# Input products are emitted as soon as a PSUM bank is free; only their evacuation waits for the phase and the places that the job needs

## The chip, the cores and the metric

One core of one Trainium2 chip runs the whole kernel in one launch. The metric is the device time of the launch in microseconds (us), the median of three runs. PE is the matrix engine, DVE the vector engine, ACT the scalar engine, POOL the general one (GpSimd), SP the engine whose queue issues nearly all DMAs.

## The reference

One layer of a streaming encoder on 2048 prompt rows and 32 sample rows of width 1024, in f32. Cut to what matters here:

```
h = layer_norm(x)
p = h @ w_in                      # 1024 -> 6160 columns: all "input products"
A: q, k, v, z of 8 heads x 64     # softmax over a band of 9 chunks of 64 keys, + learned bias
B: q, k, v, z, a, b of 8 heads    # conv of width 4 + SiLU, then gated DeltaNet in chunks of 64
                                  #   (a triangular solve per chunk, a state carried chunk to chunk)
ya = (attention * silu(zA)) @ w_branch_a
yb = (rms_norm(delta) * silu(zB)) @ w_branch_b
y  = layer_norm(ALPHA*h + (sigmoid(gA)*ya + sigmoid(gB)*yb) @ w_out)
```

The new keys, values, conv rows and states are outputs too.

## The kernel before

**Stages.** The prompt is cut in two halves of 1024 columns; the 32 sample columns ride with the second half. For each half the kernel computes the input products one block of 128 output features (a *job*) after the other, and beside them runs first phase 1 (branch B, `phase_b`) and then phase 0 (branch A, `phase_a`). So the stages in time are B of half 0, A of half 0, B of half 1, A of half 1, and last the merge with the two output projections. A few jobs, the merge gates, belong to no phase and are strewn in between as filler for PE.

**An input product.** A job's weights are split into f16 `whi` + `wlo`, and h lies as f16 `hi` + `lo`. One product block of 512 columns is 24 matmuls (`hi,whi`, `hi,wlo` eight times each, then `lo,whi` eight times) into one PSUM bank named `pj`, of which there are two. A job has two blocks in half 0 (512 + 512 columns) and three in half 1 (512 + 272 + 272). The job's `evac` then takes the bank to SBUF, mostly on ACT, and gives the bank back: `vf<-pj` for a v job of attention, `raw<-pj` for a conv job, `sig<-pj` for a gate job.

**What sets the order.** The instructions are written down by a list scheduler. Each piece of work is a Python generator (a *stream*) with a clock of its own; `Flow.run` always resumes the one whose clock is lowest, and `Engine.price` moves the clock on by a modelled cost. Streams wait for one another by `Gate` (a number of places, first come first served), `Mark` (an event) and `Queue`. The engines of the chip then run each their list in that order; what waits on the chip are the semaphores that the data need.

**The stream that writes the products** is `multiply`. It takes the next job with its split weights from `q_w`, in one fixed order. For a job of a phase (`job.key`) it then waits for `go`, which `enter` sets once the phase before is over, makes the job's `evac`, and waits for the job's places (`job.slots`). Only then does it ask for a bank (`bank["pj"]`) and emit the 24 matmuls. The places are `raw_slots` (two) for the three conv jobs of a head pair in branch B; `vf_slot` (one) and `vt_slots` (two) for v, `kst_slots` (two) for k, `q_slots` (two) for q and `z_slots` (one) for z of a head pair in branch A. While `multiply` waits, no later product can be emitted either, a filler's included.

**The other work that the text speaks of.** In branch B, `chain` carries the state over the chunks: per chunk five matmuls (`a<-state,k_bd`, `a<-state,q_bd`, `a<-r,u_bd`, `c<-vn,kd_bd`, `a<-vn,qk_bd`) with DVE and ACT steps between them, the last of which is `v_t<-a`. After eight chunks, `tail` normalises (`sqo` on ACT, `ms` on DVE and POOL, `v_t<-v_t,ms` on POOL), transposes on PE (`a<-ident,v_t`), and gates. In branch A, attention of a head pair is 8 tiles x 2 heads of scores (`a<-kst,qd` and `ql`), exponentials (`sb`), transposes (`b<-ident,sb`) and values (`c<-vt,ph` and `pl`). `job_v` ends with `rest`: the maximum of `vf`, its transposes into `vt` (`b<-ident,vs`), and in half 1 also the output rows (`b<-ident,vf`) one by one through the two `b` banks that attention uses too; its last step is the copy `v_s<-b`, after which `vf_slot` is given back.

Of the kernel before, what the change touches and what calls it, by code (L numbers as in the profile page):

```python
# [251 lines left out]
def trunk(ctx: ExitStack, tc: tile.TileContext, x_p, x_s, cache_k, cache_v, st_conv, st_gdn,  # L252
# [4 lines left out]
    flow = Flow()  # L257
# [20 lines left out]
    def mark():  # L278
        return Mark(flow)
# [8 lines left out]
    def pt(tag):  # L288

        return psum.tile([P, 512], F32, tag=tag, bufs=banks[tag], name=tag)  # L290
# [245 lines left out]
    def h_cols(half, c0, n):  # L536
        b = 0 if c0 < SPLIT else 1
        hi, lo = hT[half][b]
        o = c0 - b * SPLIT
        return hi[:, :, o:o + n], lo[:, :, o:o + n]  # L540


    class Job:
# [2 lines left out]

        def __init__(self, half, wid, src, evac=None, key=None, cols=P, blocks=None):
            self.wid = wid
            self.half, self.src, self.evac, self.cols, self.key, self.slots = half, src, evac, cols, key, ()
            self.end = self.two = False  # L550
            self.blocks = blocks or BLOCKS[half]

# [34 lines left out]
    def divide():  # L587

        while True:
# [16 lines left out]
            for i in range(2):  # L606
# [8 lines left out]
                    q_w.put((job, hi, lo))  # L615
                yield

    def multiply():

        while True:  # L620
            some, todo = [], [(0, 0)]
            while todo:
                bi, which = todo.pop(0)
                if which == len(some):
                    some.append((yield from q_w.get()))
                    job = some[which][0]
                    if which == 0:

                        todo = [(b, w) for b in range(len(job.blocks)) for w in range(1 + job.two)][1:]
                    if job.key:  # L630
                        go, make = phases[job.key[0]][job.half]
                        yield go
                        job.evac, job.slots = make[0](*job.key[1:])
                    for g in job.slots:
                        yield g
                job, wh, wl = some[which]
                c0, n, gcol = job.blocks[bi]
                tiles = range(c0 // P, (c0 + n + P - 1) // P)
                for i in tiles:
                    yield h_ready[job.half][i]  # L640
                hh, hl = h_cols(job.half, c0, n)
                yield bank["pj"]
                ps = pt("pj")
                for k in range(KD):
                    PE.matmul(ps[:, 0:n], wh[:, k], hh[:, k, :], start=(k == 0), stop=False)
                    yield
                    if job.cols == P:
                        PE.matmul(ps[:, 0:n], wl[:, k], hh[:, k, :], start=False, stop=False)
                        yield
                for i in tiles:  # L650
                    yield l_ready[job.half][i]
                for k in range(KD):
                    PE.matmul(ps[:, 0:n], wh[:, k], hl[:, k, :], start=False, stop=(k == KD - 1))
                    if k == KD - 1:
                        last = bi == len(job.blocks) - 1
                        if job.end and (bi == 0 or last):
                            h_free[0 if bi == 0 else 1].give()
                        if last:
                            w_gate.give()
                    yield  # L660
                flow.start(job.evac(bi, c0, n, gcol, ps))
                if job.end and job.half == 1:
                    if last:
                        jobs_done.done()
                        flow.start(leave())
# [34 lines left out]
    def leave():  # L700
        for _ in range(2):
            yield sig_slots
        yield front_w
        front_done.done()
# [1150 lines left out]
    phases = [[(mark(), []) for _ in range(2)] for _ in range(2)]  # L1855
# [304 lines left out]
    with tc.tile_pool(name="x0", bufs=1, reuse_waits="tile") as xp:  # L2160
        flow.start(norm_params(xp))
        flow.start(build_h(0, xp, 8))
        flow.start(fetch(marked()), 2.0)
        flow.start(setup(xp), 20.0)
        flow.start(setup2(xp), 30.0)
        flow.start(spread(), 100.0)
        flow.start(divide())
        flow.start(multiply())
        flow.run(l_ready[0][7])
    for half in range(2):  # L2170
        stack, make, done = phase_b(half)
# [9 lines left out]
        ap, stack, make, done = phase_a(half)  # L2181
# [66 lines left out]
```

## Time and profile before

| what | value |
|---|---|
| median of 3 runs | 2180.49 us (2174.0 to 2183.27) |
| the profiled execution: its time, its span | 2178.3 us, 2176.2 us |
| PE busy, matmuls | 2008.7 us (92%), 15098 |
| DVE / ACT / POOL busy | 1539.9 / 983.9 / 634.5 us |
| mean granted clock of PE | 0.971 |

The profiled execution is 2.2 us under the median. All work goes through two helpers, so nearly every row has the line L243 and is told apart by the tiles' names. PE's busy time is a union over pipelined matmuls: in a row of one instruction the time includes its overlap with the next, so the pace of a run of matmuls is read from a stretch of time, not from the mean of one.

### The profile page before, as it was taken

To read this page: it belongs to the slowest core of one execution; us is meant where nothing else is said; L and a number is where in the kernel's file an instruction comes from. 1 tells how busy PE (TensorE), PEld (TensorE's weight loads), DVE (VectorE), ACT (ScalarE), POOL (GpSimd) and SP (SyncE) were. 2 spreads that over 40 slices of the span, in tenths; PEclk is the share of its full clock that TensorE was granted. 3 is DMA by queue.
4 is the path that set the end of the run, shared out by engine and by line. 5 is a ranking of instruction groups with operands and counts; after the bars stand their busy time and mean duration, and the time that the engine had idled before them with its cause. 6 is when DMAs were issued, how large, how long until landed. Compare 5 with 4: busy or idle time off the path is not lost. (4 is left out here: it accounts for less than half of the span.)

```text
span 2176.2 us, 41392 instructions
## 1 busy us (share of the span) xinstructions
PE 2008.7 (92%) x15098; PEld 1436.2 (66%) x15098; DVE 1539.9 (71%) x4660; ACT 983.9 (45%) x2098; POOL 634.5 (29%) x708
## 2 busy tenths in 40 slices
PE   4898999999899999898999998899899998999998
PEld 4454665666465556565767776666676777988896
DVE  7689878874377657769887877437557577776676
ACT  5654545444366667554443533345556552111110
POOL 6343333322312123332233331310110214443333
PEclk9999999999999999999999999999999999999999
DMA  3223332332323223122223233231321526443331
GB/s 119 71 83 104 77 86 61 88 88 83 91 77 109 78 88 99 65 69 61 81 58 95 65 91 84 84 107 45 92 68 53 153 76 205 142 129 108 117 104 59
DMA packets 197719, 196.49 MB, mean 90 GB/s; under 512 B 79622, under 2 KB 147570, under 8 KB 197516
## 3 DMA queue, kind: packets, MB, share of 16 engines
q1 hardware_dynamic: 197516, 193.85, 30.4%
q8 instruction: 119, 1.95, 0.4%
q14 instruction: 84, 0.69, 0.1%
HBM read 135.91 MB, written 50.53 MB: 86 GB/s over the span
## 5 line engine op out<-in xcount | busy, mean ns | idle before, releaser
L243 PE MATMUL pj<-hi,whi 128*128 128x512 f16 (+2 forms) x1992 | 659.5, 346 | 16.4 <-ACT raw L243 7.8
L243 PE MATMUL pj<-hi,wlo 128*128 128x512 f16 (+2 forms) x1952 | 649.1, 345 | 0.4 <-POOL wlo L243 0.4
L243 PEld LDWEIGHTS <-whi 128*128 128x128 f16 x3984 | 412.4, 105 | 226.0 <-issue 17.7
L243 PE MATMUL pj<-lo,whi 128*128 128x512 f16 (+2 forms) x1992 | 450.2, 341 | 0.0
L243 POOL TENSOR_TENSOR wlo<-wraw,whi 128x512 f16<-128x512 f32 x192 | 227.9, 1188 | 696.7 <-ACT whi L243 421.5
L243 PEld LDWEIGHTS <-wlo 128*128 128x128 f16 x1952 | 204.7, 105 | 119.9 <-issue 20.9
L243 ACT CAST mh<-sg 128x256 fp32r<-128x256 f32 x64 | 25.9, 406 | 276.0 <-DVE sg L243 276.0
L243 DVE TENSOR_TENSOR sys_u<-sys_u,sys_t 128x60 f32<-128x60 f32 (+24 forms) x527 | 134.2, 255 | 18.5 <-DVE sys_t L243 0.2
L243 ACT ACTIVATE wraw<-wraw,w_scale 128x1024 f32<-128x1024 f32 (+1 forms) x98 | 111.5, 1137 | 63.1 <-DVE w_scale L243 62.6
L243 PE MATMUL a<-ghi,whi 128*128 128x256 f32 (+1 forms) x512 | 132.3, 289 | 7.6 <-DVE sg L243 7.4
L243 ACT CAST whi<-wraw 128x512 f16<-128x512 f32 (+1 forms) x196 | 119.3, 611 | 30.6 <-PE pj L243 28.0
L243 ACT CAST ph<-b 128x512 f16<-128x512 f32 (+2 forms) x224 | 92.9, 422 | 86.8 <-PE b L243 78.9
L243 PE MATMUL a<-ghi,wlo 128*128 128x256 f32 (+1 forms) x512 | 130.2, 285 | 0.6 <-DVE wlo L243 0.5
L243 DVE TENSOR_TENSOR pl<-b,ph 128x512 f16<-128x512 f32 (+2 forms) x224 | 106.8, 484 | 26.3 <-ACT ph L243 25.6
L243 DVE TENSOR_TENSOR sys_t<-sys_u,sys_p 128x60 f32<-128x60 f32 (+21 forms) x459 | 118.4, 258 | 4.7
L243 ACT ACTIVATE sb<-sb,mx,unit 128x640 f32<-128x640 f32 (+4 forms) x128 | 108.8, 851 | 27.7 <-DVE mx L243 25.8
L243 DVE SCALAR_TENSOR_TENSOR acc<-raw,cwT,acc 128x512 f32<-128x512 f32 x144 | 113.2, 786 | 6.0 <-ACT acc L243 5.0
L243 ACT COPY v_t<-a 128x64 f32<-128x64 f32 x132 | 27.9, 211 | 192.6 <-PE a L243 184.0
L243 POOL TENSOR_TENSOR w_scale<-w_scale,mhalf 128x1 f32<-128x1 f32 x49 | 30.3, 618 | 287.3 <-DVE w_scale L243 219.2
L243 PE MATMUL b<-ident,sb 128*128 128x128 f32 x560 | 100.0, 279 | 14.1 <-ACT sb L243 6.2
L243 PEld LDWEIGHTS a<-ghi,whi 128*128 128x128 f32 x512 | 97.7, 191 | 9.6 <-DVE sg L243 8.5
L243 PEld LDWEIGHTS a<-ghi,wlo 128*128 128x128 f32 x512 | 97.3, 190 | 1.3 <-DVE wlo L243 1.0
(356 smaller groups left out, 4270.5 us busy)
## 6 DMA issues: line engine op xcount, KB each, us to landing
wraw<-in_w_in SPq DMA_DIRECT2D x192, 256.0 KB
sg<-sig SPq DMA_DIRECT2D x112, 128.0 KB
sig<-sig SPq DMA_DIRECT2D x44, 256.0 KB
sys_p<-sol_p SPq DMA_DIRECT2D x17, 512.0 KB
x<-in_x_p SPq DMA_DIRECT2D x16, 512.0 KB
xt<-in_x_p SPq DMA_DIRECT2D x16, 512.0 KB
out_y_p<-xt SPq DMA_DIRECT2D x16, 512.0 KB
glo<-g SPq DMA_DIRECT2D x14, 512.0 KB
```

The lines of the kernel that those rows point to most:

```text
L243: r = f(*a, **k)
```

## The change

The waiting for `go` and for the places moves out of `multiply` into a stream per job, `open_job`, and a job's blocks are emitted as soon as weights, h and a `pj` bank are there. The evacuation of each block first waits for the mark `job.open`. So at most two blocks (the two banks) can stand finished in PSUM before their job is open; a third waits for a bank.

```diff
-            self.half, self.src, self.evac, self.cols, self.key, self.slots = half, src, evac, cols, key, ()
+            self.half, self.src, self.evac, self.cols, self.key = half, src, evac, cols, key
...
+    def open_job(job):
+        go, make = phases[job.key[0]][job.half]
+        yield go
+        job.evac, slots = make[0](*job.key[1:])
+        for g in slots:
+            yield g
+        job.open.done()
+
+    def evac(job, *block):
+        if job.key:
+            yield job.open
+        yield from job.evac(*block)
+
...
                     if job.key:
-                        go, make = phases[job.key[0]][job.half]
-                        yield go
-                        job.evac, job.slots = make[0](*job.key[1:])
-                    for g in job.slots:
-                        yield g
+                        job.open = mark()
+                        flow.start(open_job(job))
...
-                flow.start(job.evac(bi, c0, n, gcol, ps))
+                flow.start(evac(job, bi, c0, n, gcol, ps))
```

No matmul, vector instruction or DMA is added or taken away; the scheduler writes the same work in another order.

**Place 1: PE at the end of branch B, half 0.** `a<-ident,v_t 128x128 x4` are the transposes of the last tail of the phase, the rows above them the last chunk of the chain; `whi_5806` are the weights of the first v job of attention. Before:

```order
L243 MATMUL a_5997<-state_118,k_bd3_600 128x64
L243 MATMUL a_5999<-state_118,q_bd1_612 128x64
L243 MATMUL a_6009<-r_6001,u_bd1_624 128x64
L243 MATMUL c_6013<-vn_6011,kd_bd1_618 128x64
L243 MATMUL a_5999<-vn_6011,qk_bd3_608 128x64
L243 MATMUL a_6038<-ident_106,v_t_5307 128x128 x4
L243 LDWEIGHTS whi_5806
L243 MATMUL pj_6062<-hi00_147,whi_5806 128x512
```

The first block of the v job stands behind the transposes. After the change (`whi_5756` are the weights of the v job, `pj_5992` its second block, `whi_5914` the weights of the next job, k):

```order
L243 MATMUL pj_5992<-lo01_150,whi_5756 128x512
L243 MATMUL a_6059<-state_118,k_bd3_600 128x64
L243 MATMUL a_6064<-state_118,q_bd1_612 128x64
L243 MATMUL a_6068<-r_6066,u_bd1_624 128x64
L243 MATMUL b_6072<-w_sq_127,tiny_125 128x1
L243 MATMUL c_6074<-vn_6070,kd_bd1_618 128x64
L243 MATMUL a_6064<-vn_6070,qk_bd3_608 128x64
L243 MATMUL a_6104<-ident_106,v_t_5332 128x128 x4
L243 LDWEIGHTS whi_5914
L243 MATMUL pj_6135<-hi00_147,whi_5914 128x512
```

Both blocks of the v job now stand among the chunks of the chain, and end one chunk ahead of the transposes; between that chunk and the transposes nothing stands.

**Place 2: PE at the end of branch B, half 1.** `v_t ... 64x64` are the transposes of the last tail (the sample's); `pj_17024` before, and `pj_16995` after, are the first and the second block of the first v job. Before:

```order
L243 LDWEIGHTS whi_16556
L243 MATMUL pj_16896<-lo11_10119,whi_16556 128x272
L243 MATMUL a_16973<-ident_106,v_t_16086 64x64 x4
L243 MATMUL a_16983<-ident_106,v_t_16086 64x64 x4
L243 LDWEIGHTS whi_16757
L243 MATMUL pj_17024<-hi10_9912,whi_16757 128x512
```

After:

```order
L243 LDWEIGHTS whi_16747
L243 MATMUL pj_16995<-lo11_10190,whi_16747 128x272
L243 MATMUL a_17033<-ident_106,v_t_16212 64x64 x4
L243 LDWEIGHTS whi_16747
L243 MATMUL pj_17079<-hi11_10189,whi_16747 128x272
```

Here the first block and three quarters of the second stand ahead of the first four transposes, the rest of the second ahead of the other four, and the third block (`pj_17079`) behind them.

**Place 3: PE in branch A, half 1, where the second pair's v job begins.** `b<-ident,vf0` is one of the first pair's output rows, the other rows are its attention. Before:

```order
L243 MATMUL b_17740<-ident_106,sb_17603 128x128 x4
L243 MATMUL b_17749<-ident_106,ob_17732 128x128
L243 MATMUL b_17754<-ident_106,vf0_17049 32x128
L243 MATMUL b_17758<-ident_106,sb_17590 128x128
L243 LDWEIGHTS qd0_17324
L243 MATMUL a_17764<-kst0_17149,qd0_17324 128x320
L243 MATMUL b_17766<-ident_106,sb_17603 128x128
L243 LDWEIGHTS whi_17419
L243 MATMUL pj_17772<-hi10_9912,whi_17419 128x512
```

After:

```order
L243 LDWEIGHTS whi_17225
L243 MATMUL pj_17501<-lo11_10190,whi_17225 128x272
L243 LDWEIGHTS whi_17398
L243 MATMUL pj_17569<-hi10_9971,whi_17398 128x512
L243 LDWEIGHTS wlo_17399
L243 MATMUL pj_17569<-hi10_9971,wlo_17399 128x512
```

Before, 80 matmuls of attention and output rows stand between the last block of the first pair (`pj_17522`) and the first of the second pair. Now the second pair's first block follows the last of the first pair (`pj_17501`) at once; its second block (`pj_17653`) is spread over the attention up to 71 matmuls on, and then 85 other matmuls stand alone until the third block (`pj_17951`). At the two later pairs 99 and 87 such matmuls stood alone before, and 66 and 70 now.

## The prediction

> **What bounds the kernel now.** I read the page's busy times first, then PE's waits, then stretches of time by stage, then the stretches in which no input product runs.
>
> ```profile
> span 2176.2 us, 41392 instructions
> PE 2008.7 (92%) x15098; PEld 1436.2 (66%) x15098; DVE 1539.9 (71%) x4660; ACT 983.9 (45%) x2098; POOL 634.5 (29%) x708
> ```
>
> PE is busy for 2008.7 of 2176.2 us. The change alters no instruction, so PE's work stays, and the time can fall only by PE's idle time (167.5 us in all) and by stretches at a lower clock. The question is how much of the idle time stands where a product is held back by its phase or its places. By stage (start; B of half 0; A of half 0; B of half 1; A of half 1 up to the first pair's last product, then the other three pairs; merge), with PE's busy time first after the length, and the granted clock behind the engines:
>
> ```profile
> 0.00:37.43 37.43, 15.79 (x82) 13.61 (x83) 27.67 (x89) 19.64 (x40) 22.72 (x29) 1.00 0.42 147
> 37.43:544.38 506.95, 467.32 (x3196) 293.73 (x3195) 391.96 (x1282) 251.25 (x484) 168.75 (x212) 0.96 0.29 81
> 544.38:851.63 307.25, 293.55 (x2178) 172.36 (x2177) 192.37 (x717) 184.47 (x381) 67.40 (x69) 0.98 0.30 88
> 851.63:1402.24 550.61, 507.15 (x4141) 374.75 (x4139) 427.68 (x1361) 257.05 (x551) 166.02 (x228) 0.96 0.28 77
> 1402.24:1460.16 57.92, 51.79 (x348) 34.41 (x348) 22.07 (x60) 19.59 (x40) 14.61 (x14) 0.94 0.35 96
> 1460.16:1750.80 290.64, 272.62 (x2535) 193.00 (x2535) 181.84 (x636) 172.80 (x405) 38.78 (x34) 0.99 0.29 83
> 1750.80:2176.20 425.40, 400.45 (x2629) 354.37 (x2626) 296.32 (x523) 79.08 (x200) 156.18 (x123) 0.98 0.38 119
> ```
>
> The start (21.6 us idle) and the merge (25.0) have no job with a phase. In the two B stages 39.6 and 43.5 us are idle, but products run there almost without a break: PE stands in the middle of a block, at a chain's matmul. The waits say whom for:
>
> ```profile
> PE a L243 <- DVE r L243: 17.8, 18, 2.7
> PE a L243 <- POOL v_t L243: 14.1, 3, 6.6
> PE c L243 <- DVE vn L243: 11.3, 13, 3.3
> ```
>
> `r` and `vn` are the chain's own DVE steps, many short waits that no held-back product explains. `v_t` is the tail of a phase: three long ones. The stretches in which a job's first block comes late are eight; the last two rows are one v block after such a gap, and one block of the same size in full run:
>
> ```profile
> 544.38:556.58 12.20, 4.31 (x28) 3.49 (x26) 4.80 (x18) 4.95 (x9) 6.45 (x6) 0.75 0.28 86
> 654.67:656.35 1.68, 0.83 (x19) 0.70 (x16) 0.52 (x3) 1.59 (x3) 0.00 (x0) 1.00 0.29 79
> 719.53:724.30 4.77, 2.33 (x37) 1.73 (x38) 3.03 (x11) 1.96 (x5) 0.55 (x1) 1.00 0.39 97
> 1048.30:1052.11 3.81, 1.38 (x12) 1.14 (x12) 3.38 (x13) 2.13 (x5) 1.21 (x1) 1.00 0.34 114
> 1402.24:1409.90 7.66, 1.53 (x16) 1.42 (x17) 2.96 (x10) 2.42 (x5) 5.38 (x6) 0.82 0.36 99
> 1460.16:1477.22 17.06, 10.28 (x81) 6.41 (x81) 10.66 (x38) 10.92 (x27) 2.32 (x2) 0.90 0.25 76
> 1548.20:1563.45 15.25, 9.58 (x99) 6.58 (x98) 11.59 (x47) 10.88 (x27) 2.31 (x2) 1.00 0.29 93
> 1634.44:1647.77 13.33, 8.21 (x88) 5.38 (x89) 10.21 (x39) 10.02 (x25) 2.33 (x2) 1.00 0.36 113
> 1409.90:1417.23 7.33, 7.33 (x27) 3.02 (x27) 2.50 (x9) 0.00 (x0) 2.32 (x3) 0.72 0.22 54
> 1422.62:1427.97 5.35, 5.35 (x28) 2.56 (x26) 2.56 (x4) 1.51 (x3) 2.28 (x2) 1.00 0.15 51
> ```
>
> Length less busy time gives PE's idle time in them: 7.89, 0.85, 2.44, 2.43, 6.13, 6.78, 5.67 and 5.12, together 37.3 us. That is the pool; what the change takes from it depends on where the two early blocks land. A block of 512 columns costs 5.35 us at full clock, one of 272 columns 2.84 (5.35 x 272 / 512, an estimate).
>
> **Entry to A of half 0 (7.89 us idle).** The wait is nearly all one:
>
> ```profile
> 545.67 0.38 PE L243 MATMUL b<-w_sq,tiny 128*128 128x1 f32 x2 [0.24 <-ACT whi L243]
> 547.61 0.41 PE L243 MATMUL a<-r,u_bd 128*128 128x64 f32 x2 [0.25 <-DVE w_scale L243]
> 548.41 0.43 PE L243 MATMUL c<-vn,kd_bd 128*128 128x64 f32 x2 [0.40 <-DVE vn L243]
> 555.67 1.11 PE L243 MATMUL a<-ident,v_t 128*128 128x128 f32 x4 [6.60 <-POOL v_t L243]
> ```
>
> The tail (square, sums, POOL's power and product) takes from 549 to 555.67, and PE has nothing. The two blocks, 10.7 us, would cover it; but the scheduler gives them out at the first free bank, and place 1 shows them among the chunks, done one chunk ahead of the transposes. Both banks are then full. So the 6.60 stays, and of the 1.29 us of small waits what belongs to the last chunk: 0.24 + 0.25 + 0.40. Saved: 0.4. The price of having products beside a chunk is read from the chain's pace:
>
> ```profile
> 541.17 0.33 PE L243 MATMUL a<-state,k_bd 128*128 128x64 f32 x2
> 544.22 0.33 PE L243 MATMUL a<-state,k_bd 128*128 128x64 f32 x2
> 546.70 0.43 PE L243 MATMUL a<-state,k_bd 128*128 128x64 f32 x2
> ```
>
> 3.05 us with products between, 2.48 without: 0.57 per chunk, here for less than one chunk more than before, 0.2. Net 0.2 us. Bounds: 0 (or below it by the chain, see the rivals), and 9.9 if the blocks cover the tail after all (7.89, and 1.98 for a first block that then runs at full clock, 7.33 less 5.35). I take 0.2, by the order.
>
> **Inside A of half 0 (0.85 + 2.44).** Three stretches of other matmuls stood alone between blocks, 17, 20 and 35 of them (the middle one cost no idle time); one of 22 is left. Left idle: 3.29 x 22 / 72 = 1.0; saved 2.3, between 0 and 3.3.
>
> **The one place in B of half 1 (2.43).** A conv job's first block is held by `raw_slots`. The product can now come earlier, but its evacuation still needs the raw buffer, which DVE's conv frees (DVE is 78% busy over the stage). Between 0 and 2.43 I take half, 1.2.
>
> **Entry to A of half 1 (6.13 us idle, then a block at a low clock).**
>
> ```profile
> 1401.96 0.28 PE L243 MATMUL pj<-lo,whi 128*128 128x272 f16 x1
> 1408.37 1.60 PE L243 MATMUL a<-ident,v_t 64*64 64x64 f32 x16 [6.13 <-POOL v_t L243]
> 1411.77 0.70 DVE L243 TENSOR_SCALAR gs<-gs,w_inv 64x32 f32<-64x32 f32 x4
> 1420.05 0.49 ACT L243 ACTIVATE vf<-pj,w_inv 128x272 f32<-128x272 f32 x1 [2.09 <-PE pj L243]
> ```
>
> Here place 2 shows the blocks where the hole is: nothing of the chain is left to mix with. Before, PE waits to 1408.37, transposes, and has two blocks done at 1419.9, just ahead of the second evacuation (1420.05). After: from 1402.24 the two blocks (5.35 + 2.84 = 8.2) and the transposes (1.5) are done at 1411.9, since `v_t`, ready at 1408.37, is there when PE comes to it at about 1409.7. The new wait: the third block needs a bank, so the first evacuation. ACT's list has that behind the tail, and it waits for DVE. DVE's last step, in this profile done at 1412.47, follows the transposes and moves by their 1.3 us to 1413.8; an evacuation of 0.7 gives 1414.5. So 2.6 us of new idle time, and the third block starts at 1414.5 in place of 1419.9: 5.4 us saved. Bounds: 2.5, if the evacuation has to wait for the reads of the tail's last DMAs as well, and 8.1 (6.13 + 1.98) if it waits for nothing.
>
> The clock's share of this: in the row 1409.90:1417.23 the granted clock is 0.72 and the block took 7.33 us, against 5.35 at 1.00. [...]
>
> **The other three pairs of A, half 1 (6.78 + 5.67 + 5.12 = 17.57 idle).** Here the v job is held by `vf_slot` until the pair before has written its last row, `v_s`:
>
> ```profile
> 1476.75 0.26 ACT L243 COPY v_s<-b 32x128 f32<-32x128 f32 x1 [0.19 <-PE b L243]
> ```
>
> The product follows at 1477.22. After the change two blocks run ahead, but place 3 shows them directly behind the last product of the pair before, beside attention, where PE had work anyhow; then 85, 66 and 70 other matmuls stand alone where 80, 99 and 87 did. The hole moves more than it closes. Idle per lone matmul is 17.57 / 266 = 0.066 us, so 221 of them leave 14.6: 3.0 saved. Bounds: 0 (moved whole) and 17.6 (closed).
>
> **Other queues.** DMAs are the same in number. A job that finishes its blocks sooner frees its weight buffers sooner, so SP loads `wraw` and ACT and POOL split it earlier; ACT and POOL are busy for 45% and 29%, so I cost that at nothing; were it not covered, it would show as ACT work in front of evacuations, within the bounds above. The places that open a job (memory, DMA of `vf` and `kst` from the half before) stay where they were. In the two B stages the order is reshuffled with no trend that I can price: 0, give or take 6 us, about 15% of each stage's idle 40.
>
> **Sum.** 0.2 + 2.3 + 1.2 + 5.4 + 3.0 = 12.1 us. The profiled execution's own time is 2178.3, so 2166.2; on the scale of the median, 2180.49 - 12.1 = 2168.4, or 0.56% less. About 0.5% (10.9 us) is what a measurement of this kernel can tell from no change.
>
> **Rivals.**
> - *The holes only move.* The entry to A of half 1 gains its 5.4, all else nothing: 2175. For it speaks that in places 1 and 3 the blocks land where PE was busy already. Against it, that fewer matmuls stand alone in two of three gaps.
> - *The holes close.* All 37.3 us and two clock losses of 2.0 go: 2139. For it: the early blocks are 8.2 or 10.7 us long and each hole has at most 7.9 us of idle time. Against it: two banks are all, and they are full before the hole.
> - *Slower: the v place comes later.* In A of half 1 the output rows take turns with attention at the two `b` banks. If they fall behind, `vf_slot` comes later. In the order of the change 156 other matmuls stand between the first pair's last product and the second pair's third block, where 80 stood before its first. At the pace of the gap (17.06 us for 81 matmuls, 0.21 each) 76 more are 16 us, against 8.2 us of blocks done ahead: 7.8 lost a pair, 23 on three, less the 9.1 of the other terms: 2194. It decides from a delay of 8.2 + 9.1 / 3 = 11.2 us a pair on; against it, the two later pairs have 31 fewer and 8 more matmuls from release to release, so the delay does not recur.
> - *The chain pays.* Products ahead of a chain's matmul on PE hold it up, and the chain sets a phase's end. One more product in front of half of the 132 chunks (64 in each half, 4 of the sample), at 5.35 / 24 = 0.22 us, is 14 us: 2183, no gain. For it: 0.57 us per chunk above. Against it: only two blocks can run ahead. [...]
>
> **How the numbers follow.** The sum's case 0.45, of which four fifths end below 2169.6; holes move 0.25; holes close 0.13; place later 0.09; chain pays 0.08. Faster by over 0.5%: 0.36 + 0.13 = 0.49; within: 0.09 + 0.25 + 0.08 = 0.42; slower: 0.09. Predicted is the sum's 2168. The range goes down to 2146, most of the way to closed holes, and up to 2184, past the chain's case; outside are the late place and the last of the closed holes. The sum's own range is 2160 to 2175.
>
> **What would show it.** Right: in the profile after, PE's wait for `v_t` at the end of B of half 0 is still about 6.6 us long and that at the end of half 1 is below 1; the v block of half 1 after the transposes comes about 2.6 us behind PE's last work at granted clock 1.00; three holes of some 5 us are left in A of half 1, behind the second v block. Wrong: the wait for `v_t` gone in half 0, holes below 2 us in A of half 1 (closed), `v_s` copies more than 11 us later against the pair's first product (late place), or chunks beyond 3.05 us (chain).

## The result and the profile after

The changed kernel takes 2124.35 us (median of 4 runs, 2120.83 to 2131.39), the kernel before 2177.24 us beside it (4 runs). The ratio is 0.976, 95% interval 0.9728 to 0.9793: 2.4% faster, where the prediction had 0.56%, and below its range. The profiled execution took 2125.62 us, its span is 52.4 us shorter than before's:

```profile
span 2123.8 us, 41417 instructions
PE 1990.3 (94%) x15098; PEld 1424.6 (67%) x15098; DVE 1532.8 (72%) x4660; ACT 981.4 (46%) x2098; POOL 632.4 (30%) x708
```

PE's idle time fell from 167.5 to 133.5 us (34.0 less), and its busy time from 2008.7 to 1990.3 (18.4 less) with the same 15098 matmuls. Here are the prediction's seven stages, cut at the same products (length, then PE busy; the granted clock is the first number behind the engines):

```profile
0.00:37.54 37.54, 15.86 (x80) 13.37 (x80) 27.74 (x87) 19.64 (x40) 22.60 (x29) 1.00 0.43 147
37.54:532.99 495.45, 460.25 (x3156) 286.09 (x3157) 391.27 (x1272) 249.70 (x480) 169.37 (x211) 0.97 0.30 83
532.99:838.43 305.44, 296.17 (x2259) 177.73 (x2258) 199.85 (x742) 186.18 (x389) 65.92 (x69) 0.99 0.30 91
838.43:1374.37 535.94, 500.47 (x4097) 366.69 (x4096) 420.86 (x1347) 256.32 (x546) 166.63 (x229) 0.97 0.29 78
1374.37:1424.99 50.62, 49.44 (x349) 33.72 (x348) 20.87 (x59) 18.88 (x40) 14.62 (x14) 1.00 0.41 114
1424.99:1703.68 278.69, 271.35 (x2566) 194.32 (x2564) 181.25 (x646) 173.55 (x411) 38.24 (x34) 1.00 0.31 90
1703.68:2123.80 420.12, 396.73 (x2601) 352.69 (x2600) 290.99 (x511) 77.08 (x196) 155.00 (x123) 0.98 0.37 118
```

Length less busy time is the idle time. Against before's rows it fell by 4.4 us in B of half 0, 4.4 in A of half 0, 8.0 in B of half 1, 4.9 in the first pair of A of half 1, 10.7 in its other pairs, and 1.6 in the merge. The prediction had 0, 2.5, 1.2, 5.4 (3.4 of it idle time, the rest clock), 3.0 and 0. The rows are cut at products, and other matmuls have moved across the cuts: 40 of the chain's that stood ahead of the last product of B in half 0 now stand behind it (3196 less 3156), and 28 have left the merge for the pairs. So a stage's length is read together with its neighbour's.

Three of PE's waits after the change; the columns are the total, the number of times, and the longest:

```profile
PE a L243 <- DVE r L243: 15.0, 20, 2.1
PE c L243 <- DVE vn L243: 12.5, 20, 1.0
PE a L243 <- POOL v_t L243: 6.9, 1, 6.9
```

One wait for `v_t` is left of three (6.6, 6.1 and 1.4 us before; the prediction called all three long): that at the end of B of half 0, as forecast. The one at the end of half 1 is gone. The stretches around the v jobs (entry to A of half 0; entry to A of half 1; the two early blocks of the next pair and the hole behind them; the holes of the last two pairs):

```profile
548.78:558.80 10.02, 2.59 (x18) 2.15 (x17) 4.00 (x15) 5.44 (x9) 5.33 (x5) 0.76 0.00 1
1374.21:1379.94 5.73, 5.73 (x32) 2.98 (x30) 2.27 (x7) 2.03 (x5) 3.92 (x4) 1.00 0.48 128
1424.83:1438.93 14.10, 14.10 (x121) 9.64 (x118) 9.25 (x33) 10.32 (x23) 2.32 (x2) 1.00 0.26 77
1438.93:1447.88 8.95, 7.09 (x85) 5.28 (x86) 6.91 (x25) 5.94 (x16) 0.00 (x0) 1.00 0.17 45
1522.03:1529.06 7.03, 4.72 (x67) 3.47 (x67) 5.12 (x22) 4.30 (x12) 0.00 (x0) 1.00 0.09 23
1602.75:1610.03 7.28, 5.10 (x71) 3.90 (x72) 5.15 (x23) 5.39 (x16) 0.00 (x0) 1.00 0.39 122
```

The holes of the three later pairs have 1.9, 2.3 and 2.2 us idle, not the 5 forecast, and 85, 67 and 71 matmuls, almost the 85, 66 and 70 that the order showed. The matmuls were where they were expected; their pace was not.

One more wait was on before's list and should have been read in the prediction:

```profile
PE pj L243 <- ACT raw L243: 7.8, 2, 4.4
```

A product waits for a bank whose evacuation into a conv job's raw buffer is late. Both places are in half 1. After the change that wait is 0.4 us. Before's POOL and ACT at the first of the two places (start, duration, and in brackets the idle time ahead and what ended it):

```profile
944.77 1.72 POOL L243 TENSOR_SCALAR_AFFINE_SELECT e_in<-e_in 64x512 f32<-64x512 f32 x2 [4.67 <-DVE e_in L243]
946.55 0.19 POOL L243 COPY raw<-carry 128x3 f32<-128x3 f32 x1
...
944.13 0.63 ACT L243 ACTIVATE e<-acc 128x512 f32<-128x512 f32 x1 [2.39 <-DVE acc L243]
946.00 0.72 ACT L243 ACTIVATE acc<-raw,cwT 128x512 f32<-128x512 f32 x1 [1.24 <-DVE qk L243]
946.63 0.67 ACT L243 ACTIVATE raw<-pj,w_inv 128x512 f32<-128x512 f32 x1
...
947.35 0.38 PE L243 MATMUL pj<-hi,whi 128*128 128x272 f16 x1 [3.44 <-ACT raw L243]
```

and the same job after the change:

```profile
922.26 1.16 POOL L243 TENSOR_TENSOR wlo<-wraw,whi 128x512 f16<-128x512 f32 x1 [0.19 <-DVE acc L243]
923.36 0.19 POOL L243 COPY raw<-carry 128x3 f32<-128x3 f32 x1
...
924.34 0.72 ACT L243 ACTIVATE acc<-raw,cwT 128x512 f32<-128x512 f32 x1 [0.32 <-DVE qk_s L243]
924.97 0.67 ACT L243 ACTIVATE raw<-pj,w_inv 128x512 f32<-128x512 f32 x1
```

The job's third block waits for the evacuation `raw<-pj` of its first. Before, that evacuation stands in ACT's list behind two steps of earlier convolutions, which wait 2.39 and 1.24 us for DVE, and it follows them at once. After the change the product is done when the place comes free, so the evacuation is written into ACT's list two steps earlier, ahead of both. POOL's copy into the raw buffer also stands earlier, ahead of the selection that waited 4.67 us; but the evacuation does not wait for that copy. At another place in before, the evacuation of a job's first block starts ahead of the same job's copy:

```profile
134.34 0.69 ACT L243 ACTIVATE raw<-pj,w_inv 128x512 f32<-128x512 f32 x1 [0.87 <-PE pj L243]
...
134.65 0.65 POOL L243 COPY raw<-carry 128x3 f32<-128x3 f32 x1
```

And at the second place of the wait the copy comes 4.6 us ahead of the evacuation, which stands behind a step of ACT that waits 4.39 us:

```profile
1003.06 0.19 POOL L243 COPY raw<-carry 128x3 f32<-128x3 f32 x1
...
1007.10 0.63 ACT L243 ACTIVATE e<-acc 128x512 f32<-128x512 f32 x1 [4.39 <-DVE acc L243]
1007.63 0.67 ACT L243 ACTIVATE raw<-pj,w_inv 128x512 f32<-128x512 f32 x1
```

By its length this wait is most of the 8.0 us of half 1, and none of the 4.4 of half 0: there products waited 2.8 us before and 3.2 after, each time for POOL's `whi`. The largest wait that went in half 0 is one of the chain, which has no row after the change:

```profile
PE c L243 <- DVE w_scale L243: 4.4, 2, 4.0
```

Why it is gone is not shown.

### The profile page after: what moved, and what is told of

The parts are those of the page before. It is cut to its first block, busy times and chain, and to the rows that moved or that the text cites. A ratio compares the mean times of both kernels' runs of the same rounds, so it can differ in the third digit from the quotient of the medians.

```text
span 2123.8 us, 41417 instructions
## 1 busy us (share of the span) xinstructions
PE 1990.3 (94%) x15098; PEld 1424.6 (67%) x15098; DVE 1532.8 (72%) x4660; ACT 981.4 (46%) x2098; POOL 632.4 (30%) x708
## 5 line engine op out<-in xcount | busy, mean ns | idle before, releaser
L243 PE MATMUL pj<-hi,whi 128*128 128x512 f16 (+2 forms) x1992 | 647.6, 341 | 9.1 <-POOL whi L243 3.2
L243 PE MATMUL pj<-hi,wlo 128*128 128x512 f16 (+2 forms) x1952 | 638.2, 340 | 1.0 <-POOL wlo L243 1.0
```

Source lines behind the costliest of these rows:

```text
L243: r = f(*a, **k)
```

## The experiments

Stages are named by the input product blocks in order of time, counted from 0: B of half 0 ends with block 61, the entry to A of half 0 with 69, A of half 0 with 99; B of half 1 is 114 to 194, the entry to A of half 1 is 195 to 206, its later pairs with the gates 207 to 248, then comes the merge. Each experiment is an edit of the changed kernel unless said otherwise.

**Half of the change at a time.** Four kernels, by phase of the wait and by branch:

```
only_phase   +  if not begun: wait for nothing   else: yield job.open     # ahead only until the phase begins
only_places  +  yield phases[job.key[0]][job.half][0]                     # waits for the phase, not for the places
only_a       +  if job.key[0] == 1: yield job.open                        # B jobs wait as before
only_b       +  if job.key[0] == 0: yield job.open                        # A jobs wait as before
```

> A job runs ahead only while its phase has not begun; once it has, it waits for its places before its products. Held products: the entry to A of half 1 gains its 6 to 7 us, the holes of half 1 stay: 7 to 12 us under before. Order luck: the same entry, and up to 10 us either way from the B stages, though nothing of them is let run ahead but their first job.

> A job waits for its phase before its products, but no longer for its places. Held products: everything but the entries, so 40 to 46 us under before, with the 6 us hole at the entry to A of half 1 back. Order luck: the three holes of A of half 1 closed to 7 to 9 us as in the profile after (12 to 15 us gained), the rest within 10 us of before.

> Only the jobs of branch A run ahead; a job of branch B waits for phase and places before its products, as in the kernel before. Theory 'held products' (every gain comes from a product that is no longer held, and adds up by stage: in the profile after, 3.5 us inside A of half 0, 6.7 at the entry to A of half 1, 12 in its pairs and 5 in the merge came there): about 27 us under the kernel before, and the two B stages as long as before. Theory 'order luck' (the B stages gained 10 and 11 us because the list was shuffled): the A part as above, the B stages anywhere within 10 us of before.

> Only the jobs of branch B run ahead. Held products: B of half 0 and of half 1 gain their 10 and 11 us, the three holes of 13 to 17 us in A of half 1 are all there: some 20 to 25 us under the kernel before. Order luck: within 10 us of before, either way.

Beside 2179.46 us for before: only_phase 2173.11 (ratio 0.9966, 0.9945 to 0.9986), only_places 2134.25 (0.98, 0.9756 to 0.9843), only_a 2146.05 (0.9846, 0.9811 to 0.9881), only_b 2165.16 (0.9941, 0.9921 to 0.996). The gains, 6.4 and 45.2, or 33.4 and 14.3, add up to 51.6 and 47.7 us of the 53: the parts are nearly additive, and the places in branch A are the largest. Of the forecasts of 'held products' only_places met its 40 to 46 us; only_phase gained less than its 7 to 12, only_a more than its 27, and only_b, with 14.3, lies between the 20 to 25 of that theory and the 10 of 'order luck'. By stage, the 7 us at the entry to A of half 1 come only where jobs run ahead of the phase, the 12 us of the later pairs only where A jobs run ahead of their places, and a B of half 1 that is shorter by 11 us and more (481.0 and 482.8 us against 493.9) only where B jobs do; only_phase has 488.9. In only_a, whose B jobs wait as before, B of half 0 is 6.8 us longer than in before. One part is an interaction: in only_b and only_places B of half 0 ends 8 and 13 us earlier, but the entry to A is then 70 us long (58 before). The products end ahead of the chain, the v job may not start, and 40 matmuls more of the chain stand in the entry (273 against 233), where the granted clock is 0.83 (0.91 before).

**A of half 1 alone.** All other jobs wait as before, so PE's list is the same as before's up to the end of B of half 1.

```
+  if job.key[0] or not job.half: yield job.open
```

> Products run ahead in A of half 1 alone; in all other stages each job waits before its product, as before, and PE's list is the same as before up to the end of B of half 1. So it is the prediction's two terms for that stage alone (entry 5.4 and pairs 3.0, 8.4 us: 2171). Theory 'each early block covers its own time, at the start of the hole': entry 6 to 8 and pairs 11 to 13 as in the changed kernel, some 19 us, 2155 to 2163. Rival 'prediction's sizes': 2168 to 2174. Rival 'the gain of that stage needs the earlier ones': below 5 us, 2174 or more.

2158.96 us against 2177.82 (ratio 0.9911, 0.988 to 0.9942): 18.9 us. The rival with the prediction's sizes falls. The stages (up to the end of B of half 1; first pair; other pairs; merge):

```profile
0.00:1410.93 1410.93, 1295.19 (x9591) 861.56 (x9592) 1041.32 (x3447) 712.27 (x1454) 424.63 (x537) 0.96 0.29 82
1410.93:1461.63 50.70, 49.27 (x346) 33.17 (x344) 21.15 (x60) 19.27 (x40) 14.60 (x14) 1.00 0.41 113
1461.63:1742.00 280.37, 273.04 (x2565) 195.17 (x2564) 181.41 (x646) 173.45 (x411) 38.29 (x34) 0.99 0.31 89
```

50.70 and 280.37 us stand against before's 57.92 and 290.64: 7.2 and 10.3. The first row says something else. Before's is

```profile
0.00:1402.24 1402.24, 1283.82 (x9590) 854.46 (x9590) 1039.68 (x3447) 712.41 (x1454) 424.88 (x537) 0.96 0.29 83
```

The same list took 8.7 us more in this execution, with 11.4 us more of PE busy time and 2.7 less idle, and with about 126 us at half clock in place of 102. These two executions of one list differ by that much in one stretch, with about 24 us more at half clock in the longer; so a single difference of 5 or 10 us in a long stage carries little.

**How many blocks ahead.** In A of half 1 only the first block of a v job runs ahead, in two lists (the second with the hop cost of the reshuffles below).

```
+  if bi and job.half and job.key and job.key[0] == 0 and job.key[2] == 0: yield job.open
```

> As the changed kernel, but in A of half 1 a v job multiplies only its first block ahead; the second waits for the job's opening. The changed kernel gained 11.9 us over before in the three later pairs of that stage, where the prediction had 3.0 by counting idle time per lone matmul. Theory 'ramp': the idle time of before's three holes stands at their start (4.47, 3.70 and 3.54 us of it in the first half, with 26, 24 and 19 matmuls; 2.31, 1.96 and 1.57 in the second half, with 56, 75 and 69), so one block of 5.35 us laid over the start brings most: 8 to 10 of the 11.9 us, a time of 2126 to 2129. Rival 'each block covers its own time': half, 6 us, 2130. Rival 'idle per lone matmul': at most 1.5 of the 11.9 us, 2134 to 2136.

> One block ahead in the v jobs of A of half 1, two elsewhere, in the list that hop cost 0.18 gives (two ahead: 2124.4 us; three later pairs, gates and merge 704.3 us; idle time in the pairs 8.6 us). Theory 'each block covers its own time': the two together give up 5 to 10 us of their gain, 2129 to 2135, and the pairs' idle time is 10 to 13 us. Rival 'ramp' (one block brings most): 2124 to 2128 and below 10 us of idle time. Rival 'idle per lone matmul': 2134 or more and 15 us or more of idle time.

one_ahead: 2134.88 us (2133.12 to 2136.51), where two blocks ahead had 2124.35; one_ahead_hop18: 2123.83 (2121.31 to 2127.35) where two had 2124.37. PE's idle time in the later pairs went from 18.0 (none ahead) to 11.5 (one) to 7.3 (two) in the first list, and from 19.2 to 8.9 to 8.6 in the second. So by idle time one block brings 61% and 97% of what two bring, which speaks for the ramp. By time it brought all in one list and missed 10.5 us in the other, which is the number of 'idle per lone matmul', though that theory's 15 us of idle time are not there. Between the two profiled executions of the first list 6.5 us are idle time and 4.1 are PE's busy time. The reason for the ramp is in before's first hole, cut in two:

```profile
1460.16:1468.69 8.53, 4.06 (x26) 2.28 (x25) 4.66 (x19) 6.77 (x17) 2.32 (x2) 0.99 0.47 144
1468.69:1477.22 8.53, 6.22 (x56) 4.13 (x56) 6.01 (x20) 4.15 (x11) 0.00 (x0) 0.81 0.03 8
```

Attention of a new pair starts with few matmuls ready: 26 and 4.47 us idle, then 56 and 2.31. The early blocks lie over the first part, and what is left alone is the second.

**Mere reshuffles.** Before and after with the planner's hop cost at 0.22 and at 0.18 in place of 0.20 us; the work is the same.

```
-HOP_PE, HOP, HOP_SAME = 0.1, 0.2, 0.12
+HOP_PE, HOP, HOP_SAME = 0.1, 0.22, 0.12        (hop18: 0.18)
```

> The kernel before, with one cost of the planner (the hop from one engine to another) 0.22 in place of 0.20 us, which reshuffles all lists and changes no work. It measures what a mere reshuffle is worth. Theory 'held products': a reshuffle is worth little against the change, 2171 to 2190 (before is 2179). Rival 'luck of the order': reshuffles move the time by 15 us or more either way, so the two B stages' gains of some 10 us each are no effect of the change.

> The changed kernel with the same altered cost, 0.22 in place of 0.20 us. Theory 'held products': 2117 to 2137, and 45 to 62 us below the reshuffled kernel before, with both B stages at least 6 us shorter than there. Rival 'luck of the order': the gap to the reshuffled kernel before is below 35 us, and at least one B stage is as long as there.

> The kernel before with the planner's hop cost at 0.18 in place of 0.20 us. Theory 'held products, each list worth some 10 us either way': 2168 to 2190, B of half 1 at least 489 us, the three later pairs of A of half 1 at least 290. Rival 'luck of the order': B of half 1 or those pairs as short as with early products, 484 or 283 us or less.

> The changed kernel with the planner's hop cost at 0.18 in place of 0.20 us: a second reshuffle. Theory 'held products, each list worth some 10 us either way': 2124 to 2150, and 25 to 55 us below the kernel before with the same reshuffle; by stage, B of half 1 (blocks 114 to 194) at most 489 us and the three later pairs of A of half 1 with their gates at most 284, as in every kernel so far whose products run ahead there (477.8 to 488.5 and 278.7 to 282.7). Rival 'luck of the order': the gap is below 20 us and these two stages overlap with those of held products (488.9 to 494.3 and 290.2 to 298.6).

before_hop 2178.63 us (ratio to before 0.9989, 0.9963 to 1.0016), after_hop 2146.35 (0.9854, 0.9803 to 0.9906); before_hop18 2173.86 (0.996, 0.9932 to 0.9987), after_hop18 2124.37 (0.9728, 0.969 to 0.9766). In the three lists the change is worth 53, 32 and 49 us. It is an effect of the change and no luck, but its size hangs on the list. after_hop missed all of its bounds: 2137 us, a gap of 45 us, and B stages at least 6 us shorter than in before_hop (they are 3.0 and 3.4 us shorter). Its gap is below the 35 us of 'luck of the order', whose other condition, a B stage as long as there, did not come. before_hop18's B of half 1, 486.8 us, fell between the two theories' bounds, and after_hop18's later pairs, 285.6 us, between theirs. In the profiled executions of the three lists PE's idle time falls by 34.0, 9.2 and 23.0 us, and its busy time by 18.4, 15.6 and 30.9.

**Late evacuations.** The products of B jobs stay early; the evacuations are written no sooner than in the kernel before, relative to the opening. Three lists.

```
     yield job.open
+    if job.key[0] == 1: yield job.open.at + 24 * job.blocks[0][1] / 2400.0
```

> As the changed kernel, but in the two B stages the planner gives out a job's evacuations (with the copies on POOL that open the job) no sooner than 5.12 us of its own clock after the opening, which is where they stood when the product itself waited for the opening; the products stay early. Theory 'place of the evacuation': the 11.2 us of B in half 1 (blocks 114 to 194) and the 9.7 of B in half 0 come because evacuation and opening stand earlier in the lists of ACT and POOL, ahead of steps that wait (in before POOL's copy into the raw buffer stood behind a selection with 4.67 us of waiting, ACT's evacuation behind an activation with 4.39 us): then the B stage of half 1 falls back to within 4 us of before, and the time is 2136 to 2146. Rival 'the early product itself': the gain stays, B of half 1 at -8 us or better against before, 2122 to 2130.

> The kernel with late evacuations in the B stages (products early, evacuations and opening copies no sooner than 5.12 us of the planner's clock after the opening), in the list that hop cost 0.22 gives. Theory 'place of the evacuation': both B stages are as long as with held products (B of half 0, blocks 14 to 61: 425 to 437 us; of half 1: 487 to 494), 2150 to 2165. Rival 'the early product itself': as with early products (416 to 422, and 481 to 489), 2135 to 2150.

> The same late evacuations, in the list that hop cost 0.18 gives. Theory 'place of the evacuation': B of half 0 at 425 to 437 us and of half 1 at 487 to 494, 2135 to 2150. Rival 'the early product itself': 416 to 422 and 481 to 489, 2118 to 2132.

2142.97, 2158.37 and 2122.44 us (the changed kernel with the same lists: 2124.35, 2146.35, 2124.37). The first two totals are in the range of 'place of the evacuation', the third in that of 'the early product itself'; by stage no theory holds: in the first list half 0 is as long as with held products (432.9 us) and half 1 as short as with early ones (477.8), in the second half 1 is long (498.4) and half 0 lies between (423.0), in the third both are short (411.5 and 485.9). One row is the same in all three, and stands between the 7.8 us of before and the 0.4 of after:

```profile
PE pj L243 <- ACT raw L243: 4.3, 1, 4.3
```

In all three this wait is that of before's first place, and again it is ACT's list that holds the evacuation. In the first list:

```profile
936.88 0.18 POOL L243 COPY raw<-carry 128x3 f32<-128x3 f32 x1
...
940.98 0.63 ACT L243 ACTIVATE e<-acc 128x512 f32<-128x512 f32 x1 [2.39 <-DVE acc L243]
942.36 0.72 ACT L243 ACTIVATE acc<-raw,cwT 128x512 f32<-128x512 f32 x1 [0.76 <-DVE qk L243]
942.99 1.04 ACT L243 ACTIVATE raw<-pj,w_inv 128x512 f32<-128x512 f32 x2
```

POOL's copy is done 5.9 us ahead of the evacuation. The wait is 6.2 to 7.9 us in the six kernels whose B jobs wait, at most 0.8 in six of the seven whose products and evacuations are early, and 5.9 in the last of these, after_hop, which also has the longest B of half 1 of them. So the place of the evacuation in ACT's list decides that wait: with the early evacuation of the same list it is 0.4 and 0.8 us in two lists, and 5.9, at the second place, in after_hop's. Whether it decides the rest of the B stages' gain is left open.

Means (least to greatest) of a stage's length over the profiled executions of all kernels with two product banks (the clock's ladder below apart), by what is held there; one_ahead and one_ahead_hop18 are left out of the pairs. The second row adds the entry behind B of half 0, since matmuls of the chain move into it; 'early' there are the kernels in which the products of both run ahead:

| stage | held | early | difference |
|---|---|---|---|
| B of half 0, 14 to 61 | 432.6 (425.2 to 437.4) | 419.4 (416.5 to 422.2) | -13.2 |
| the same with the entry to A, 14 to 69 | 488.5 (485.6 to 494.1) | 478.4 (470.6 to 488.0) | -10.1 |
| B of half 0, late evacuations | | 422.5 (411.5 to 432.9) | -10.1 |
| A of half 0, 70 to 99 | 252.5 (249.3 to 260.0) | 244.8 (242.8 to 245.7) | -7.7 |
| B of half 1, 114 to 194 | 491.6 (486.8 to 494.3) | 484.0 (481.0 to 488.5) | -7.6 |
| B of half 1, late evacuations | | 487.4 (477.8 to 498.4) | -4.2 |
| entry to A of half 1 | 56.2 (53.6 to 57.9) | 50.8 (48.1 to 55.2) | -5.4 |
| later pairs of A of half 1 | 294.7 (290.2 to 298.6) | 280.8 (278.7 to 285.6) | -13.9 |

In only_b and only_places, where products run ahead in B of half 0 but the v job waits for its phase, stage and entry together are 491.5 and 487.7 us, as long as with held products.

**A third product bank.**

```
-banks = {"pj": 2, "a": 3, "b": 2, "c": 1}
+banks = {"pj": 3, "a": 2, "b": 2, "c": 1}
```

> The changed kernel with three product banks in place of two, and two in place of three of the bank kind that the gated delta chain and the merge use. Theory 'depth': a v job of half 1 then runs ahead with all its three blocks, which covers what is left of idle time in A of half 1 (8.5 us in the changed kernel: 1.2 at the entry, 7.3 in the pairs) and some of the 7.4 us at the entry to A of half 0: 2108 to 2119. Rival 'the chain pays for the bank': chain and merge wait for one bank fewer, 2130 to 2160, with the B stages and the merge longer than in the changed kernel (418, 483 and 420 us).

2201.78 us (ratio to before 1.0082, 1.0052 to 1.0112): 77 us slower than with two. The direction of 'the chain pays' was right, and so was the longer merge (437.9 us against 420.1); its size and its longer B stages were not. The B stages are shorter than in the changed kernel, 401.3 and 445.2 us against 418.4 and 482.8; the entries to A are longer (half 0, half 1):

```profile
516.13:615.34 99.21, 87.39 (x444) 56.93 (x442) 31.55 (x118) 26.77 (x56) 23.26 (x22) 0.76 0.24 67
1359.75:1478.27 118.52, 99.66 (x573) 74.77 (x572) 53.29 (x182) 26.86 (x68) 20.98 (x19) 0.74 0.24 62
```

against 59.7 and 50.6 us. Products went first, and the chain, with one `a` bank fewer, was left over at the end of the phase with little beside it and a clock of 0.76 and 0.74. Stage and entry together are 22 and 30 us longer. Of the 76 us between the two profiled executions 47 are PE's busy time, with 179.7 us at half clock against 87.1. The edit gives the products a bank and takes one from the chain, so it does not show which of the two decides.

**The clock by itself.** Behind the end of the changed kernel, bursts of 56 matmuls (12.26 us at granted clock 1.00) with waits of known length between them.

```
+for steps in ((), (256,), (512,), (512, 128), ... (512, 1024, 1024, 512)):
+    for _ in range(7):
+        56 x PE.matmul(ps[:, 0:512], w, x);  copies of these widths on ACT;  the last one writes w
```

> The changed kernel, and behind its end ten groups of seven bursts of 56 matmuls (128x512, 16 bit, some 12 us each); between bursts PE waits for a chain of copies on ACT, which is made longer from group to group, from about 0.5 to about 4.5 us. The whole is some 950 us longer for that, and only the bursts' clock is read. In the kernels so far the half-clock stretches start on a grid of 3.41 us, and come behind slices of that grid in which PE was idle for about 1.75 us or more. Theory 'half a slice': no burst behind a wait below 1.7 us starts at half clock, of those behind waits of 2 to 3.4 us a growing part does, and all do from about 3.5 us on. Rival 'a whole idle slice': none does below 3.4 us, and all only from 6.8 us on, so hardly one in this run.

| wait, us | 0.43 | 0.86 | 1.07 | 1.40 | 1.72 | 2.15 | 2.59 | 2.80 | 3.23 | 3.88 |
|---|---|---|---|---|---|---|---|---|---|---|
| bursts with a half-clock stretch | 0 of 6 | 0 of 7 | 0 of 7 | 0 of 7 | 0 of 7 | 3 of 7 | 5 of 7 | 6 of 7 | 7 of 7 | 6 of 6 |

Five of them, each row one wait and the burst behind it (waits of 1.72, 2.15, 2.15, 2.80 and 3.23 us, the length less the busy time):

```profile
2585.69:2599.67 13.98, 12.26 (x56) 5.41 (x56) 0.00 (x0) 1.51 (x3) 0.00 (x0) 1.00 0.00 0
2599.67:2615.77 16.10, 13.95 (x56) 5.83 (x56) 0.00 (x0) 1.94 (x3) 0.00 (x0) 0.89 0.00 1
2615.77:2630.17 14.40, 12.26 (x56) 5.41 (x56) 0.00 (x0) 1.94 (x3) 0.00 (x0) 1.00 0.00 0
2868.20:2883.26 15.06, 12.26 (x56) 5.41 (x56) 0.00 (x0) 2.56 (x4) 0.00 (x0) 1.00 0.00 0
2933.49:2950.66 17.17, 13.95 (x56) 5.84 (x56) 0.00 (x0) 2.98 (x4) 0.00 (x0) 0.90 0.00 1
```

The burst behind the same wait of 2.15 us took 1.69 us more in the second row (13.95 us against 12.26, granted clock 0.89 over the row), and nothing more in the third. All half-clock stretches of this run began on one grid of 3.41 us. Where at least 2.07 us of a wait fell into one slice of it, a half-clock stretch followed (27 of 27); where at most 2.03 did, none (41 of 41). 'Half a slice' is confirmed, with the edge between 2.03 and 2.07 us here, 0.6 of one; the rival falls.

## Why the prediction was wrong

- **"PE's work stays": wrong, 18.4 us.** The matmuls stay, their clock does not (mean granted clock 0.971 before, 0.98 after). In before's clock records 129.7 us lie at half clock (granted 0.5) in 27 stretches, after it 87.1 in 16; half of the 42.6 us between them, 21, is about the 18.4 that PE's busy time fell (the half is an estimate: in the ladder a burst with 3.41 us of it took 1.69 us more). Over the sixteen kernels with two product banks (the ladder apart) busy time falls by 0.45 us for each us less at half clock (correlation 0.96). The step that failed: the prediction counted the clock at two v blocks only, with 2.0 us in its sum, and took a wait of 2.6 us to cost no clock. No run shows that term: in the ladder half clock followed 5 of 7 waits of 2.59 us, and all 27 waits of which at least 2.07 us fell into one slice of the grid; the wait that came in its place was 1.2 us long, with granted clock 1.00 behind it.
- **B stages at 0 (1.2 for one place): wrong.** Their idle time fell by 12.4 us. In half 1 (8.0 us) the step that failed is pricing only a job's first block. The third block was held too, through a bank that an evacuation had not given back, and the row for it was on the list of waits (7.8 us, 0.4 after). "The places that open a job stay where they were" failed with it: the evacuation moved up in ACT's list. In half 0 (4.4 us) no such wait shrank: there the term "no trend that I can price: 0" was too small, and the cause stays open.
- **The three pairs at 3.0: mis-sized.** By idle time they gave 10.7 us, alone (only_a1) 18.02 less 7.33, the same. Idle time per lone matmul treats a hole as even, and it is not: before's first hole has 0.17 us of it per matmul in its first half and 0.04 in its second.
- **Entry to A of half 1 at 5.4: right.** 7.3 us in this pair of executions, 5.4 as the mean over lists. The idle time in front of the third block is 1.2 us (forecast 2.6), at granted clock 1.00.
- **Entry to A of half 0 at 0.2: right in kind.** The wait for `v_t` is still there (6.9 us; before's longest 6.6), since both banks are full before it; the entry is 59.7 us in place of 58.0, with 40 matmuls more.
- **Inside A of half 0 at 2.3:** 3.6 us in this pair of executions; the idle time of the whole stage with its entry fell by 4.4, where 2.5 were forecast.
- **The rivals.** "Holes close" was nearest, and true of A of half 1, where the idle time fell from 24.2 to 8.5 us; it lacked the B stages and the clock. The late place did not happen: the first pair's `v_s` comes 5.6 us later against its first product, under the 11. Nor did the chain pay: its last four chunks of half 0 stand 3.05 us apart, the pace that the prediction read beside products.

By terms: of the 12.1 us forecast 10.1 were idle time and 2.0 clock. In this pair of executions 34.0 us of idle time went; B of both halves missed 11.2, the pairs 7.7, A of half 0 1.9, the merge 1.6, and the entry in half 1 1.5. The clock's 18.4 make up the 52.4.

## What to carry to other kernels

A held producer can cost more than the wait in front of it. Here its evacuation was written later into ACT's list, behind steps that waited 2.39 and 1.24 us, and the job's third block waited 3.44 us for it. So read the waits of every block of a job, not of the first alone. When a change closes waits of about 2 us and more on PE, add as an estimate the ladder's 1.69 us for each of which at least 2.07 us fall into one slice of the clock's grid (27 of 27 there), and before believing a gain of a few us in one stage, time the same edit in two or three reshuffled lists.

## What was not expected of the hardware

In the ladder, with its dense matmuls, all half-clock stretches began on one grid of 3.41 us, as did before's 27 and after's 16. A slice of it with at least 2.07 us of a wait was followed by half clock in 27 of 27 cases, one with at most 2.03 in none of 41. In the traces of before and after, which have mixed matmuls, the slice behind one at full clock with 1.75 us or more of idle time was at half clock in 31 of 31 cases, behind one with less in 12 of 1146. In other kernels of this record some slices with up to 1.98 us were not followed by one, so the edge is not sharp there. The grid's lines lie 0.82 us behind multiples of 3.41 us from the kernel's first instruction in before, 1.00 us in after, and 2.35 us in only_a1. Up to the end of B of half 1 before and only_a1 run the same list, and only_a1 had 11.4 us more of PE busy time there, with about 126 us at half clock against 102; that this comes from where the grid lay is the author's estimate, and no run shows it by itself.
